# Seven column tiles instead of six accumulate while adaLN's weights stream in; adaLN keeps one PSUM bank

## The chip, the cores and the metric

The kernel runs on one core of a Trainium2 chip. The metric is the device time of one execution, in microseconds, the median of several runs. TensorE multiplies (PE in the profile, its weight loads PEld), VectorE (DVE) and GpSimd (POOL) do elementwise work, ScalarE (ACT) does activations and casts, SyncE (SP) starts every DMA. TensorE writes its sums to PSUM, eight banks of 512 float32 columns on 128 partitions.

## The reference

One layer of a hybrid decoder, in float32, on 2048 prompt tokens and 8 single-token samples. The part that the change touches is the head of it:

```python
shift, scale, gate = adaln(c, w_c, b_c)              # silu(c) @ w_c + b_c, split in three
h = rmsnorm(x, g_pre) * (1.0 + scale[:, None, :]) + shift[:, None, :]
proj = h @ w_in                                      # 2048 -> 5 x 1024
u_a, v_a, z_a, x_b, z_b = jnp.split(proj, [D_A, 2 * D_A, 3 * D_A, 3 * D_A + D_B], axis=-1)
```

Behind it come a gated mixing of chunks of 128 tokens (A), an S5 state space scan (B), a product with `w_out` (2048 x 2048), a second RMSNorm, and the residual. The outputs are the new rows, the normalised v rows of the samples, and the S5 states.

## The kernel before

The tokens are cut into four blocks of 512 (the last has the 8 samples too), the 40 x 128 output columns of `w_in` into column tiles, the 2048 input rows into 16 K tiles (KT). A float32 product is made of three: weights and activations are each split into a rounded high part and the rest (`hi`, `lo`), and `mm3` (lines 95 to 99) multiplies hi by hi, hi by lo and lo by hi. So a K tile of one column tile (`kstep`) is three matmuls of 512 columns. The weights arrive raw by DMA, 512 KB at a time (`wraw`, line 106), and `wpieces` (line 111) makes two pieces of each: ACT casts the high part (line 90), DVE or POOL subtracts it (line 85). A load is either half of one column tile (`whalf`, eight K tiles) or a quarter of two (`wpair`, four K tiles of each).

**The startup** (`startup`, line 1244) cannot make h before adaLN's shift and scale are there, and those need 32 MB of `w_c`: 64 loads of 512 KB (`raw`, eight buffers), four for each of the 16 K tiles. So h is made K tile by K tile, and the first NG = 6 column tiles of the first block accumulate at once, each in a PSUM bank of its own, four of the tag `acc` and two of `aux`. Step s of the loop does four things. Six `kstep`s use K tile s - 2. `ada_ss2` turns the sums of K tile s - 1 (`ada_turn`: four small matmuls into a bank `adat`; DVE adds the biases, lines 289 and 291, into `shiftT` and `GT`), and `hscale` (x times R on DVE, line 342) and `hmake` (ACT: x, line 348, and hi; DVE: lo) make its h. The `w_c` loads of K tile s are multiplied (`ada`, line 271) in two bursts, behind the third and the sixth `kstep`, into a bank `ada` that is opened at the step's start, and `ada_copy` (line 275) takes the sums out to SBUF. Each `ada` starts the load of the buffer that it has freed. The weights of the six column tiles come as pairs through three raw buffers (`wraw2`): loaded in steps 2, 6 and 10, split in steps 4 and 5, 8 and 9, 12 and 13. All this is in `manual_schedule`: each engine, and SP with its DMAs, does its part in the order of the code. An instruction whose buffer is not free yet waits, and what is behind it on its queue waits too.

**Behind the startup** a planner orders the engines by the order of the code and its own estimates. `phase1_rest` does the other column tiles of the block one by one, in two halves of eight K tiles. For each half it calls `half`, which does work that is spread over the tiles: one of 16 steps of the next block's statistics (`stats`: load x, square on ACT, add on POOL, line 338; the 17th call makes R of it, `rms_wide`), from the ninth tile on a share of S5's preparation (`s5_mats`, on POOL above all), and at the ninth tile S5's lanes (`s5_lanes`, on DVE). Then `group_start` begins the next block: its h is made with R (`hgen`, lines 364 to 366) while two column tiles accumulate.

Of the kernel before, what the change touches and what calls it, by code (L numbers as in the profile page):

```python
# [27 lines left out]
G = 64  # L28
GC = 16
P = 64  # L30
KT = D // 128
# [26 lines left out]
def ranges(b):  # L58

    return [(0, TB)] if b < NB - 1 else [(0, 256), (256, 264)]  # L60


class Builder:
# [38 lines left out]
    def wsplit(self, src, raw_pool=None, raw_tag="wraw", raw_bufs=3, pool=None, tags=("whi", "wlo"), bufs=NW, engs=None):  # L102

        return self.wpieces(self.wraw(src, raw_pool, raw_tag, raw_bufs), pool, tags, bufs, engs)

    def wraw(self, src, pool=None, tag="wraw", bufs=3):
        raw = (pool or self.wp).tile([128, 1024], F32, tag=tag, bufs=bufs, name=self.nm("wraw"))
        self.SP.dma_start(raw if len(src.shape) == 2 else raw.rearrange("p (a b) -> p a b", a=2), src)
        return raw
# [1133 lines left out]

    def startup(self, st, NG, ntl):

        I, V, G = self.I, self.V, self.G
        raws, pair = {}, {}
        NS = 4 * KT
        def raw(i):
            if i < NS:  # L1250
                raws[i] = self.wraw(I["wss"][i // 4][:, i % 4 * 4 : i % 4 * 4 + 4, :].rearrange("p k m -> p (k m)"), st, "sraw", NR_)
        ws = [[] for _ in range(NG)]
        def wraw(g, kq):
            pair[g, kq] = self.wraw(self.wpair(I["win"], ntl[1][g], kq), st, "wraw2", 3)
        def wsplit(g, kq):
            a, b = self.wpieces(pair.pop((g, kq)), pool=st, tags=("swh", "swl"), bufs=NG + 2, engs=(V, G))
            ws[g].append(a)
            ws[g + 1].append(b)
        xs = [self.xload(self.hl, "hl", 0, k, NHL) if k < KT - 1 else self.xload(self.tp, "t", 0, k, NT) for k in range(KT)]
        self.constants1()  # L1260
        for i in range(NR_):
            raw(i)
        for g in (0, 2, 4):
            wraw(g, 0)
        ssq = self.tile_()
        for k in range(KT):
            self.stat_add(st, xs[k], ssq, k, TB, V)
        R = self.R[0]
        self.sel = self.cp.tile([128, 9], F32, name="sel")
        V.tensor_add(self.sel, self.ident[:, 0:9], self.ident[:, 32:41])  # L1270
        for i in (64, 96):
            V.tensor_add(self.sel, self.sel, self.ident[:, i : i + 9])
        def ada(ps, i):
            self.ada_mm(ps, raws.pop(i), i % 4)
            raw(i + NR_)
        ps = self.ada_open()
        ada(ps, 0)
        def more():
            ada(ps, 1)
            ada(ps, 2)  # L1280
        self.rms_bcast(ssq, TB, R, more)
        ada(ps, 3)
        V.tensor_scalar(self.bcT[:, 16:32], self.bcT[:, 16:32], 1.0, None, op0=ALU.add)
        sb = self.ada_copy(ps)
        self.hscale(xs[0], R, 0)
        wsplit(0, 0)
        self.ada_ss2(0, sb)
        self.h = [self.hmake(xs[0], 0, 0)]
        wsplit(2, 0)
        ps = self.ada_open()  # L1290
        for q in range(4):
            ada(ps, 4 + q)
            if q == 2:
                wsplit(4, 0)
        sb = self.ada_copy(ps)
        acc = [self.accs(0) if g < 4 else [self.ps.tile([128, 512], F32, tag="aux", bufs=4, name=self.nm("acc"))] for g in range(NG)]
        for s in range(2, KT + 2):
            if s < KT:
                ps = self.ada_open()
            prev = sb  # L1300
            if prev is not None:
                self.hscale(xs[s - 1], R, 0)
            sb = None
            for q in range(NG):
                if q < NG and s >= 2:
                    self.kstep(acc[q], ws[q][0], s - 2, self.h[s - 2], ranges(0), s == 2, s == KT + 1)
                    if (s - 2) % 4 == 3:
                        ws[q].pop(0)
                if q == 1 and prev is not None:
                    self.ada_ss2(s - 1, prev)  # L1310
                if s < KT and q in (2, NG - 1):
                    for a in range(2):
                        ada(ps, 4 * s + q // 3 * 2 + a)
                if s < KT and q == NG - 1:
                    sb = self.ada_copy(ps)
                if q == 2 and prev is not None:
                    self.h.append(self.hmake(xs[s - 1], 0, s - 1))
                if s < KT:
                    if s % 4 == 2 and s < KT - 4 and q % 2 == 0:
                        wraw(q, s // 4 + 1)  # L1320
                    if (s % 4, q) in ((0, 3), (1, 2), (1, 4)):
                        wsplit(0 if q == 3 else q, s // 4)
            if s == KT:
                w = self.wcol(I["win"][ntl[1][NG]])
        return w, acc


    def build(self):
        nc, tc, I, V, G, SP = self.nc, self.tc, self.I, self.V, self.G, self.SP
# [24 lines left out]
        self.R = [self.cp.tile([128, TB + ND], F32, name="R0")]  # L1354
        cm_st, st = self.pool("startup")
        self.constants(st)
        NG = 6
        nta, ntb = self.order(0), self.order(1)
        with tc.manual_schedule():
            w, acc = self.startup(st, NG, nta)  # L1360
# [32 lines left out]
        pair = lambda ntl: lambda hf: [self.wsplit(self.wpair(I["win"], ntl[1][0], 0))] if hf else []  # L1393
# [65 lines left out]
        y, ws = y0, ws0  # L1459
        for b in range(NB - 1):  # L1460
            y, ws = self.phase3(b, ws, y)
        self.lo_engs = [V, V, V, G]
        self.ggr = []
        y, ws = self.phase3(NB - 1, ws, y)
# [75 lines left out]
```

## Time and profile before

| | us |
|---|---|
| median of three runs | 2908.93 |
| lowest and highest | 2904.92, 2912.47 |
| the profiled execution | 2908.74 |
| its span, first to last instruction | 2906.9 |
| TensorE busy in it | 2833.2 (97%) |
| DVE, ACT, POOL busy | 1619.7, 1066.7, 1056.5 |

The profile shows one execution. An engine's busy time counts its instructions from start to end; matmuls overlap in the pipeline, so a busy TensorE may still be slower than it could be, and the distance from one start to the next tells its pace. A line such as `ACT whi L90 <- DMA wraw` says that the instruction of line 90 waited for that transfer. A wait is put down to what came last.

### The profile page before, as it was taken

The page shows a single profiled execution, that of the slowest core. Times are in us where ns is not written, and L with a number is a line of the kernel's source. Part 1 is how long each engine was busy: PE and PEld are TensorE (multiplying, and loading weights), DVE is VectorE, ACT ScalarE, POOL GpSimd, SP SyncE. Part 2 cuts the span into 40 slices and gives each one's busy share as a digit, 9 for nine tenths or more (in the row PEclk, how much of TensorE's full clock was granted, in tenths as well). Part 3 has the DMA queues.
Part 4 walks back from the last instruction along what each step waited for, and adds up shares of the span by engine and source line. Part 5 has one row for each costly group of instructions (what it writes and reads, how often), then busy time and mean ns, then how long its engine had stood idle before and what let it go on. Part 6 is the DMA issues. An engine that isn't in the chain of part 4 may idle for free.

```text
span 2906.9 us, 44350 instructions
## 1 busy us (share of the span) xinstructions
PE 2833.2 (97%) x15804; PEld 2377.5 (82%) x15804; DVE 1619.7 (56%) x2976; ACT 1066.7 (37%) x2008; POOL 1056.5 (36%) x973
## 2 busy tenths in 40 slices
PE   6999999999999999999999999999999999999997
PEld 4676777777999999988888888888888888888986
DVE  4467646557442737465546735582741274473866
ACT  3333444434233232333334332433243343434543
POOL 1128463663341232323232233223234345263442
PEclk9999999999999999999999999999999999999999
DMA  9897988988887373846476565647483365474676
GB/s 356 287 235 203 277 240 236 265 237 235 191 210 202 106 232 127 260 142 201 154 226 192 154 200 179 214 126 234 138 253 102 101 178 177 126 229 120 195 237 219
DMA packets 456559, 581.14 MB, mean 200 GB/s; under 512 B 216593, under 2 KB 303121, under 8 KB 456337
## 3 DMA queue, kind: packets, MB, share of 16 engines
q1 hardware_dynamic: 456338, 578.32, 66.6%
q8 instruction: 124, 2.03, 0.3%
q14 instruction: 97, 0.79, 0.1%
HBM read 466.87 MB, written 102.66 MB: 196 GB/s over the span
## 4 chain that ended last, share of the span: by engine, by line
PE 77%; DVE 11%; DMA 5%; issue 3%; POOL 1%; SPq 1%; ACT 1%; DVEq 0%; ACTq 0%; POOLq 0%
PE acc L97 23%; PE acc L99 22%; PE acc L98 22%; DMA x<-in_xT 2%; DVE wlo L85 2%; DVE Ub L894 2%; PE ada L271 2%; DVE lo L366 1%; DVE x L364 1%; PE mix L526 1%; DVE sct L904 1%; DVE Ub L903 1%; DVE sct L902 1%; PE acc L1223 1%; DVE Ub L905 1%
## 5 line engine op out<-in xcount | busy, mean ns | idle before, releaser
L97 PE MATMUL acc<-hi,whi 128*128 128x512 f32 (+2 forms) x3200 | 1130.0, 355 | 5.4 <-DVE t L85 2.1
L98 PE MATMUL acc<-lo,whi 128*128 128x512 f32 (+2 forms) x3200 | 1120.6, 350 | 11.6 <-DVE lo L366 9.6
L99 PE MATMUL acc<-hi,wlo 128*128 128x512 f32 (+2 forms) x3200 | 1120.1, 350 | 2.3 <-DVE wlo L85 1.9
L85 DVE TENSOR_TENSOR wlo<-wraw,whi 128x512 fp32r<-128x512 f32 x626 | 549.8, 886 | 806.2 <-ACT whi L90 788.5
L90 ACT CAST whi<-wraw 128x512 fp32r<-128x512 f32 x960 | 580.9, 620 | 1115.3 <-PE acc L98 785.6
L85 POOL TENSOR_TENSOR wlo<-wraw,whi 128x512 fp32r<-128x512 f32 x334 | 472.3, 1416 | 1053.6 <-ACT whi L90 955.2
L97 PEld LDWEIGHTS acc<-hi,whi 128*128 128x128 f32 x3200 | 602.4, 189 | 100.5 <-issue 18.2
L98 PEld LDWEIGHTS acc<-lo,whi 128*128 128x128 f32 x3200 | 603.3, 189 | 91.7 <-DVE lo L366 13.7
L99 PEld LDWEIGHTS acc<-hi,wlo 128*128 128x128 f32 x3200 | 602.5, 188 | 89.5 <-DVE wlo L85 4.9
L97 PE MATMUL acc<-yhi,whi 128*128 128x512 f32 (+1 forms) x1024 | 377.5, 369 | 2.8 <-DVE o L1069 2.8
L99 PE MATMUL acc<-yhi,wlo 128*128 128x512 f32 (+1 forms) x1024 | 375.7, 368 | 1.9 <-POOL wlo L85 1.9
L98 PE MATMUL acc<-ylo,whi 128*128 128x512 f32 (+1 forms) x1024 | 376.3, 368 | 0.0
L97 PEld LDWEIGHTS acc<-yhi,whi 128*128 128x128 f32 x1024 | 193.8, 189 | 38.6 <-DVE o L1069 3.6
L99 PEld LDWEIGHTS acc<-yhi,wlo 128*128 128x128 f32 x1024 | 193.3, 189 | 36.5 <-POOL wlo L85 2.5
L98 PEld LDWEIGHTS acc<-ylo,whi 128*128 128x128 f32 x1024 | 193.7, 189 | 34.5 <-issue 0.7
L894 DVE SCALAR_TENSOR_TENSOR Ub<-Ub,apow 128x128 f32<-128x128 f32 (+6 forms) x384 | 143.0, 435 | 2.5 <-ACT Ub L881 2.2
L983 POOL TENSOR_TENSOR sg<-sg,zbl 128x264 f32<-128x264 f32 x64 | 54.7, 854 | 191.1 <-DVE sg L982 133.0
L364 DVE SCALAR_TENSOR_TENSOR x<-x,GT,R 128x512 f32<-128x512 f32 x96 | 88.8, 940 | 31.1 <-DMA x<-in_xT 30.8
L365 ACT ACTIVATE hi<-x,shiftT 128x512 fp32r<-128x512 f32 x96 | 68.5, 723 | 95.0 <-DVE x L364 87.7
L90 ACT CAST hh<-hr 128x264 fp32r<-128x264 f32 x64 | 26.4, 413 | 190.9 <-DMA hr<-Ub 99.7
L1072 POOL TENSOR_TENSOR ossq<-ossq,osq 128x512 f32<-128x512 f32 (+1 forms) x60 | 81.2, 1354 | 32.5 <-ACT osq L1065 32.3
L338 POOL TENSOR_TENSOR ssq<-ssq,t 128x512 f32<-128x512 f32 (+1 forms) x45 | 61.7, 1372 | 83.1 <-ACT t L337 70.8
(286 smaller groups left out, 2798.3 us busy)
## 6 DMA issues: line engine op xcount, KB each, us to landing
wraw<-in_win SPq DMA_DIRECT2D x320, 512.0 KB
wraw<-in_wout SPq DMA_DIRECT2D x128, 512.0 KB
xr<-XB SPq DMA_DIRECT2D x128, 272.0 KB
x<-in_xT SPq DMA_DIRECT2D x128, 256.0 KB
wraw<-in_wss SPq DMA_DIRECT2D x64, 512.0 KB
XB<-t SPq DMA_DIRECT2D x64, 256.0 KB
wraw<-in_wgt SPq DMA_DIRECT2D x32, 512.0 KB
MQ<-qh SPq DMA_DIRECT2D x128, 128.0 KB
```

Source lines behind the costliest of these rows:

```text
L85: eng.tensor_tensor(out, a, b, op=ALU.subtract)
L90: self.S.copy(hi, raw)
L97: mm(acc, whi, xhi, start=start, stop=False)
L98: mm(acc, whi, xlo, start=False, stop=False)
L99: mm(acc, wlo, xhi, start=False, stop=stop)
L271: self.T.matmul(ps[k * 32 : k * 32 + 32, 0:256], self.stat[:, q * 4 + k, :], raw[:, k * 256 : k * 256 + 256], start=q == 0, stop=q == 3)
L338: add_eng.tensor_tensor(ssq[:, 0:n], ssq[:, 0:n], sq[:, 0:n], op=ALU.add)
L364: V.scalar_tensor_tensor(xt, xt, self.GT[:, k, 0:1], R[:, 0:TB], op0=ALU.mult, op1=ALU.mult)
L365: S.activation(hi[:, 0:TB], xt, AF.Identity, bias=self.shiftT[:, k, 0:1])
L894: V.scalar_tensor_tensor(o, i, f, o, op0=ALU.mult, op1=ALU.add)
L983: self.G.tensor_tensor(sg, sg, zb, op=ALU.mult)
L1072: eng.tensor_tensor(ssq[:, 0:nn], ssq[:, 0:nn], sq[:, 0:nn], op=ALU.add)
```

## The change

NG becomes 7, so a seventh column tile accumulates in the startup, in a third bank of `aux`. One bank of `aux` is left for adaLN's sums and their turn, in alternation: `ada_open` moves from the step's start to the first burst, and the first burst moves from behind the third `kstep` to behind the fourth, since the turn of the K tile before must be read first. A burst still is two loads, eight K tiles of `w_c`. The seventh tile has no partner; its weights come in halves: the first is loaded in step 1 and split ahead of the loop, the second is loaded in step 7 and split in step 9. There are ten buffers for split pieces where there were eight. The line that loads pairs (`if s % 4 == 2 and s < KT - 4 and q % 2 == 0: wraw(q, s // 4 + 1)`) is not touched. `phase1_rest` of the first block starts one tile further on.

```diff
         def wraw(g, kq):
-            pair[g, kq] = self.wraw(self.wpair(I["win"], ntl[1][g], kq), st, "wraw2", 3)
+
+            src = self.wpair(I["win"], ntl[1][g], kq) if g < NG - 1 else self.whalf(I["win"][ntl[1][g]], kq // 2)
+            pair[g, kq] = self.wraw(src, st, "wraw2", 3)
         def wsplit(g, kq):
-            a, b = self.wpieces(pair.pop((g, kq)), pool=st, tags=("swh", "swl"), bufs=NG + 2, engs=(V, G))
+            a, b = self.wpieces(pair.pop((g, kq)), pool=st, tags=("swh", "swl"), bufs=NG + 3, engs=(V, G))
             ws[g].append(a)
-            ws[g + 1].append(b)
+            ws[g + 1 if g < NG - 1 else g].append(b)
...
         for q in range(4):
             ada(ps, 4 + q)
+            if q == 0:
+                wraw(NG - 1, 0)
             if q == 2:
                 wsplit(4, 0)
         sb = self.ada_copy(ps)
+        wsplit(NG - 1, 0)
...
         for s in range(2, KT + 2):
-            if s < KT:
-                ps = self.ada_open()
...
                 if q == 1 and prev is not None:
                     self.ada_ss2(s - 1, prev)
-                if s < KT and q in (2, NG - 1):
+                if s < KT and q in (3, NG - 1):
+                    if q == 3:
+                        ps = self.ada_open()
                     for a in range(2):
-                        ada(ps, 4 * s + q // 3 * 2 + a)
+                        ada(ps, 4 * s + q // 4 * 2 + a)
...
                         wsplit(0 if q == 3 else q, s // 4)
+                    if (s, q) == (7, 5):
+                        wraw(NG - 1, 2)
+                    if (s, q) == (9, 5):
+                        wsplit(NG - 1, 2)
...
-        NG = 6
+        NG = 7
```

## Rows read from the trace of the kernel before

**Rows 1.** Busy by stretch: PE, PEld, DVE, ACT, POOL; clock, DMA share, GB/s

```profile
0.00:20.00 20.00, 0.45 (x8) 0.23 (x8) 11.98 (x23) 11.70 (x18) 0.20 (x4) 1.00 0.89 292
20.00:30.00 10.00, 8.53 (x52) 5.26 (x44) 4.85 (x20) 0.00 (x0) 0.00 (x0) 1.00 1.02 379
30.00:40.00 10.00, 7.82 (x63) 4.05 (x64) 5.75 (x10) 5.48 (x10) 4.30 (x3) 1.00 1.04 409
...
40.00:137.00 97.00, 97.00 (x741) 62.69 (x741) 39.32 (x79) 28.75 (x46) 13.20 (x9) 1.00 0.91 332
...
210.00:300.00 90.00, 80.82 (x400) 59.59 (x399) 68.77 (x78) 36.50 (x75) 74.70 (x92) 0.98 0.76 216
```

**Rows 2.** Timeline of TensorE, one step of the startup: start, duration, instruction

```profile
51.63 0.51 PE L282 MATMUL adat<-sel,t 128*128 128x9 f32 x4
...
52.86 1.07 PE L271 MATMUL ada<-wraw,cstat 128*32 128x256 f32 x16
...
54.20 0.39 PE L98 MATMUL acc<-lo,whi 128*128 128x512 f32 x1
54.43 0.40 PE L99 MATMUL acc<-hi,wlo 128*128 128x512 f32 x1
...
59.89 1.07 PE L271 MATMUL ada<-wraw,cstat 128*32 128x256 f32 x16
```

**Rows 3.** Timeline of DVE in the same step

```profile
52.32 0.28 DVE L291 TENSOR_SCALAR GT<-adat,c_bcT,c_gpre 128x9 f32<-128x9 f32 x1
```

**Rows 4.** Waits of SP's queue, 0 to 200 us: total, times, longest

```profile
SPq L108 <- PE ada L271: 59.8, 28, 3.4
```

**Rows 5.** Timeline of SP and ACT: the first pairs' loads and the first cast

```profile
19.43 2.89 SPq L108 DMA_DIRECT2D wraw<-in_win  x3
...
30.91 1.14 ACT L90 CAST whi<-wraw 128x512 fp32r<-128x512 f32 x2 [14.20 <-DMA wraw<-in_win]
```

**Rows 6.** Timeline of POOL, DVE and TensorE, 32 to 41 us

```profile
32.13 1.28 POOL L85 TENSOR_TENSOR wlo<-wraw,whi 128x512 fp32r<-128x512 f32 x1 [31.68 <-ACT whi L90]
...
37.02 0.41 DVE L275 COPY t<-ada 128x256 f32<-128x256 f32 x1
37.36 1.42 DVE L342 TENSOR_TENSOR x<-x,R 128x512 f32<-128x512 f32 x1
...
38.83 0.27 DVE L291 TENSOR_SCALAR GT<-adat,c_bcT,c_gpre 128x9 f32<-128x9 f32 x1
40.64 0.69 DVE L85 TENSOR_TENSOR lo<-x,hi 128x512 fp32r<-128x512 f32 x1 [1.53 <-ACT hi L90]
...
37.96 0.48 PE L97 MATMUL acc<-hi,whi 128*128 128x512 f32 x1
...
38.83 1.07 PE L271 MATMUL ada<-wraw,cstat 128*32 128x256 f32 x16
```

**Rows 7.** Timeline of SP and ACT: a load that is used at once

```profile
257.72 0.38 SPq L108 DMA_DIRECT2D wraw<-in_win  x1
...
260.21 0.62 ACT L90 CAST whi<-wraw 128x512 fp32r<-128x512 f32 x1 [0.28 <-DMA wraw<-in_win]
```

**Rows 8.** TensorE behind a wait: timeline, and busy by stretch as in rows 1

```profile
280.87 0.50 PE L98 MATMUL acc<-lo,whi 128*128 128x512 f32 x1 [2.53 <-DVE lo L366]
...
282.00:285.30 3.30, 3.30 (x14) 1.87 (x13) 3.30 (x4) 0.00 (x0) 3.06 (x4) 0.51 0.64 160
```

**Rows 9.** Timeline of POOL: the split of step 4's pair

```profile
55.23 1.34 POOL L85 TENSOR_TENSOR wlo<-wraw,whi 128x512 fp32r<-128x512 f32 x1 [17.00 <-ACT whi L90]
```

**Rows 10.** Timeline of TensorE and DVE around the next block's R

```profile
256.36 0.50 PE L158 MATMUL ssum<-sqh,ones 128*128 128x512 f32 x1 [0.64 <-ACT sqh L90]
...
271.83 0.69 DVE L145 SCALAR_TENSOR_TENSOR R<-t,R 128x512 f32<-128x512 f32 x1
...
273.05 6.20 DVE L364 SCALAR_TENSOR_TENSOR x<-x,GT,R 128x512 f32<-128x512 f32 x4
...
277.62 0.71 PE L97 MATMUL acc<-hi,whi 128*128 128x512 f32 x2
```

## The prediction

> **What bounds the kernel now.** I read the table of busy time by stretch first, because the change touches one stage. From 40 to 137 us, where six column tiles accumulate beside adaLN, TensorE is busy for all of its 97.00 us [rows 1]. Next the list of what SP's queue waits for: up to 200 us it waits 28 times for adaLN's matmuls, 59.8 us together [rows 4]. So the weight loads run ahead of TensorE and wait for it to give buffers back, and TensorE sets the pace, although the DMA share is 0.91 [rows 1]. The timeline shows the step that repeats: bursts at 52.86 and 59.89 are one step apart, 7.03 us [rows 2]. In it lie 18 matmuls of 512 columns, 0.23 us from start to start (54.20 to 54.43), two bursts of about 1.0 us, a turn of 0.4 us and the passages between them [rows 2]. There is no hole for a seventh tile to fill.
>
> **Part by part. The seventh tile itself: 0.** It brings 48 matmuls, 48 x 0.233 = 11.2 us, into the startup, and takes the same 48 out of the column tiles behind it. A step grows from 7.03 to 7.03 + 3 x 0.233 = 7.73 us. TensorE has no free time to hide them in, so this is a move, not a gain. The count of bursts, turns and passages stays.
>
> **One bank for sums and turn: 0 in a settled step.** A burst may now start only when DVE has read the turn. In the settled step the turn starts at 51.63 [rows 2] and DVE's second sum ends at 52.32 + 0.28 = 52.60 [rows 3], 0.97 us later. In the new order the turn (0.36 us) and two K tiles (2 x 0.7) stand ahead of the burst, 1.8 us, so 0.8 us are spare. Without that cover (DVE held up) the price is whatever DVE is late, and that happens once, next. The Trainium skill (PSUM — Partial Sum Buffer, section PSUM bank collisions raise a hardware error) says that TensorE and VectorE must not touch one bank in the same partitions at once. By that rule the overlap in [rows 6], where the burst and DVE's GT read both start at 38.83, is lost; by the row alone nothing would be lost, and the sum would be 4.8 us smaller, since the burst would not ask for DVE.
>
> **The seventh tile's first weights: 4.8 us.** Its first load is put into SP's order behind the thirteenth adaLN load, and into a pool of three buffers, so it waits for the split of the first pair, whose GpSimd half ends at 32.13 + 1.28 = 33.41 [rows 6]. Then it queues. How long shows the first pair: its load is issued at 19.43 and its cast starts at 30.91 after 14.20 us of waiting [rows 5]. Ahead of it and with it were 16 x of 0.262 MB, eight adaLN loads and itself of 0.524 MB, and 0.17 MB of constants: 9.1 MB. Moved by 30.91 were 20 x 0.292 + 10 x 0.379 + 0.91 x 0.409 = 10.0 MB [rows 1]. So loads land about in order, 0.9 MB behind. For the new load 13.3 MB stand in order (the same, two more pairs, five more adaLN loads, itself), so it lands at 14.2 MB; by 40.00 13.7 MB are moved, hence at 41.1 us.
>
> Its split stands in ACT's, DVE's and GpSimd's order ahead of all that step 2 needs: on DVE behind it wait x times R, both sums, and lo; on ACT hi. From 41.1: cast 0.62, wlo 0.69, x times R 1.42 beside a busy GpSimd (37.36 to 38.78), sums 0.32 (to 38.83 + 0.27 = 39.10) [rows 6]: 44.15, with the gaps between engines 44.3 us. TensorE reaches the burst after two K tiles from 37.96, at 39.5 [rows 6]; it stands there 4.8 us. The K tile of step 3 needs lo, in the trace of before 41.33 - 39.10 = 2.2 us behind the sums [rows 6], so at 46.5; TensorE gets there after a burst, three K tiles and a burst, at 48, so nothing more is late. Bounds: if the load lands as its own bytes end (13.3 MB, 38.9 us) and x times R takes 0.69, 1.9 us; if it lands 1.4 us later, 6.2 us.
>
> **TensorE's clock behind that wait: 1.6 us.** In the trace of before TensorE waits 2.53 us until 280.87, and the granted clock over the 3.3 us from 282.0 to 285.3 is 0.51, that is 1.2 GHz [rows 8]. That loses 1.6 us. The first 40 us of the trace hold the clock at 1.00 through shorter gaps [rows 1], so the bounds are 0 and 1.7. The Trainium skill (TensorE: Matmul & The Clock Gate, section HAM oscillation — how this bites in real kernels) says that an array that stands idle is put back to the half rate; by it 1.6 is due, by the early rows 0.
>
> **Three loads that nobody reads: 2.5 us.** The line that loads a pair in steps 2, 6 and 10 asks for an even q, and q = 6 is now one. So in each of these steps the seventh tile is loaded once more; no split takes these loads (that of step 6 is replaced by the one of step 7). They cost 1.6 MB of DMA, which hides, since TensorE sets the pace. But each needs a fourth buffer of three, which comes free only with the split of the first pair two steps later, and SP's queue stands there, with every adaLN load behind it. That split ends on GpSimd at 55.23 + 1.34 = 56.57 [rows 9], 4.9 us after its turn at 51.63. The eight adaLN buffers last to the end of that step; the next burst is due one step on, 1.8 + 7.7 = 9.5 us after the turn, its second load 0.5 us later. From the release two loads are ahead of its second one: a load alone takes from 257.72 to 260.21, 2.5 us, to be used [rows 7], and each further 0.524 MB at 0.4 MB/us 1.3 us. That is 4.9 + 0.05 + 2.5 + 2 x 1.3 = 10.1 against 10.0: hardly late. With the 0.9 MB lag of the busy start (2.2 us) it is 1.4 us late. Step 7's load waits besides for the dead one to land: 0 to 0.9 more. Three times 0.1 to 1.4 and this: 0.3 to 5.1; I take 2.5, the middle, as neither row is nearer.
>
> **Behind the startup: 5 us.** The statistics of the next 512 tokens are stepped once per half column tile from the first tile behind the startup on, so they now begin and end one tile (11.2 us of TensorE) later against the work that is left; S5's preparation keeps its tile. In the trace of before the sum's matmul runs at 256.36, R is done at 271.83 + 0.69 = 272.5, DVE starts on x at 273.05, and TensorE, through with its last tile at 277.62 [rows 10], waits for lo until 280.87 [rows 8]. So R leads by 5.1 us and is late all the same: 8.4 us lie between it and the first lo. Now the sum's matmul opens the last tile, 277.62 - 11.2 = 266.4, and with the same 16.1 us R comes at 282.5: 10 us later. The last tile has only one pair to split where the one before it had four halves' pieces, so DVE should need less than 16.1 us; at 11, about what R's eleven DVE operations of 0.69 [rows 10] and three subtractions make, it comes at 277.4 and costs 5. Bounds: -2, if the planner that orders this part finds better places, and 10. I take 5, near the middle and from the rows of DVE's own chain.
>
> **The sum** goes against the profiled execution, 2908.74 us (span 2906.9), which is 0.2 us under the median: 4.8 + 1.6 + 2.5 + 5 = 13.9, so 2922.6 us. By the bounds: 0.2 to 23, that is 2909 to 2932.
>
> **Rivals. A, hidden:** the load jumps the queue as the lone one does (2.5 us [rows 7]): issued at 33.5, landed by 36, sums by 39.4, no wait, no clock loss; the dead loads are late by 0.3 and the planner catches the statistics. It decides at a landing of 36.3 us. Time 2909 to 2912, no measurable change. Against it stands the first pair's 11.5 us in the queue [rows 5].
> **B, faster:** behind the startup one tile fewer is to be split and loaded (1.05 MB, four casts, four subtractions) in a stage where TensorE lacks 90.00 - 80.82 = 9.2 us between 210 and 300 [rows 1]. If that goes by more than the startup's prices, the kernel gains; with A's startup and all of it, 2900. It decides where the lost waits pass the 8.9 us of the startup. Against it: what TensorE waits for there is S5's preparation and R, which start no earlier.
> **C, much slower:** S5's lanes, the constants and the statistics all start at the startup's end, and have a tile less to hide behind. If R is the full 10 us late and half again as much falls on S5's preparation, the time is 2908.7 + 8.9 + 15 = 2932.6; it decides where DVE needs all of the 16.1 us again.
>
> **How the numbers follow.** Forecast 0.55, A 0.20, B 0.07, C 0.18. A measurement of this kernel tells about 0.3% from no change, 8.7 us. Of the forecast's spread (+6 to +20) I put three quarters above that, 0.41; with C slower is 0.59. A and the rest of the forecast are same, 0.34; faster is B, 0.07. The range takes in A and C's own time, and leaves out B and what lies beyond C: 2908 to 2933.
>
> **What the profile after would show.** In_win loads 323 instead of 320. A step of 7.7 us. One wait of TensorE of about 5 us near 40 us, with DVE as releaser, at adaLN's burst, and the granted clock at a half behind it. Three waits of SP of some 15 us for a split, and TensorE late at a burst one step later. R done no more than 2 us before the last tile's end. The prediction is wrong if the load lands before 37 us, if TensorE's idle time before the startup's end grows by less than 5 us, or if the stretch from there to the end of the next group's start shrinks.

## The result, and the profile after

The changed kernel takes 2931.76 us (median of four runs, 2929.62 to 2934.45) where the kernel before took 2906.93 beside it (2903.51 to 2912.47). The ratio is 1.0085, with a 95% interval of 1.0072 to 1.0098: 24.7 us slower (21 to 28). The forecast was 2922.6 us, slower, in a range to 2933. The sign and the places were right, and two terms of the sum were far too small. Of all the executions behind this document one, of run 3 below, took 9297 us; it is in no ratio.

The profiled execution of the changed kernel took 2930.59 us, its span is 2928.8 us. From its page, busy time by engine, the group of adaLN's matmuls (busy time and mean, then idle time ahead and its releaser), and the DMA issues:

```profile
PE 2844.1 (97%) x15804; PEld 2380.6 (81%) x15804; DVE 1621.2 (55%) x2974; ACT 1065.8 (36%) x2008; POOL 1050.8 (36%) x975
...
L271 PE MATMUL ada<-wraw,cstat 128*32 128x256 f32 x768 | 63.9, 420 | 28.4 <-DMA wraw<-in_wss 24.4
...
wraw<-in_win SPq DMA_DIRECT2D x323, 512.0 KB
```

The work is the same but for three loads more. To see where the time went, take two marks that both kernels pass: the first accumulator taken out of PSUM (line 397, the startup's end) and a taking out in the second block, behind the group start (line 419). The kernel before:

```profile
140.32 1.63 ACT L397 CAST t<-acc 128x512 fp32r<-128x512 f32 x3
...
439.39 0.59 ACT L419 ACTIVATE t<-acc 128x512 f32<-128x512 f32 x1
```

and the kernel after:

```profile
163.27 1.98 ACT L397 CAST t<-acc 128x512 fp32r<-128x512 f32 x3 [0.26 <-PE acc L99]
...
461.07 0.59 ACT L419 ACTIVATE t<-acc 128x512 f32<-128x512 f32 x1
```

The first mark comes 23.0 us later. Of the seventh tile's 48 matmuls 45, 10.5 us, were moved ahead of it (the last three come behind the first accumulator's end), so the startup has lost 12.5 us. The second mark, behind the same work in both kernels, comes 21.7 us later, so 9.2 us more are lost between the two; behind it the distance stays near 22 to the end. These two numbers are given below for each run, as **startup** and **behind**.

**The startup.** The turn of adaLN's sums (line 282) starts once a step. From turn to turn before: 7.13, then 6.99 to 7.04 in every step. After, from step 2 on: 13.79, 7.73, 7.74, **11.75**, 7.73, 7.72, 7.69, **11.03**, 7.69, 7.73, 7.70, **9.89**, 7.72, 7.72. So ten steps are 7.0 + 0.7 us, as forecast, and four are longer by 6.0 (step 2 takes 7.82 in a run below where nothing waits), 4.0, 3.3 and 2.2 us: 15.5 in all. The loads at the front came through earlier in this execution (TensorE's first wait for them is 17.5 us against 19.6 before), which gives some 2 to 3 us of it back.

TensorE's waits from 20 to 165 us (us in total, times, longest), then SP's up to 170 us, where [rows 4] had 59.8 us for adaLN's matmuls:

```profile
PE ada L271 <- DMA wraw<-in_wss: 6.9, 8, 1.7
PE acc L97 <- DVE GT L291: 3.1, 1, 3.1
```

```profile
SPq L108 <- DVE wlo L85: 54.0, 5, 16.6
...
SPq L108 <- PE ada L271: 23.3, 17, 3.5
```

SP now waits most for a split of weights, 54.0 us, and only 23.3 us for adaLN's matmuls.

Step 2 on TensorE's timeline, ACT's cast of the seventh tile's weights and DVE's sum beside it, and the busy time of the stretch (PE, PEld, DVE, ACT, POOL; clock, DMA share, GB/s):

```profile
34.83 0.61 PE L282 MATMUL adat<-sel,t 128*128 128x9 f32 x4 [1.21 <-DVE t L275]
...
42.63 0.77 PE L97 MATMUL acc<-hi,whi 128*128 128x512 f32 x1 [3.12 <-DVE GT L291]
...
48.62 0.51 PE L282 MATMUL adat<-sel,t 128*128 128x9 f32 x4
```

```profile
39.13 1.14 ACT L90 CAST whi<-wraw 128x512 fp32r<-128x512 f32 x2 [5.63 <-DMA wraw<-in_win]
...
42.22 0.27 DVE L291 TENSOR_SCALAR GT<-adat,c_bcT,c_gpre 128x9 f32<-128x9 f32 x1
```

```profile
42.00:48.30 6.30, 5.67 (x24) 3.25 (x25) 2.21 (x6) 1.43 (x2) 0.00 (x0) 0.50 1.04 398
```

The cast waits for the load, DVE's split and sums come behind it, and TensorE stands 3.12 us until GT is read. Then the granted clock is 0.50, 1.2 GHz, for some six microseconds; the rest of the 6.0, 2.9 us, is that.

The first of the three long steps, on SP, GpSimd and TensorE:

```profile
45.33 1.18 SPq L108 DMA_DIRECT2D wraw<-in_wss  x2
61.33 0.33 SPq L108 DMA_DIRECT2D wraw<-in_win  x1
61.71 13.14 SPq L108 DMA_DIRECT2D wraw<-in_wss  x12
```

```profile
59.95 1.36 POOL L85 TENSOR_TENSOR wlo<-wraw,whi 128x512 fp32r<-128x512 f32 x1 [18.33 <-ACT whi L90]
```

```profile
64.09 0.51 PE L282 MATMUL adat<-sel,t 128*128 128x9 f32 x4
...
67.84 0.64 PE L271 MATMUL ada<-wraw,cstat 128*32 128x256 f32 x8 [1.73 <-DMA wraw<-in_wss]
69.01 1.08 PE L271 MATMUL ada<-wraw,cstat 128*32 128x256 f32 x8 [0.54 <-DMA wraw<-in_wss]
...
75.84 0.51 PE L282 MATMUL adat<-sel,t 128*128 128x9 f32 x4
```

```profile
69.00:72.40 3.40, 3.39 (x14) 2.10 (x15) 0.58 (x1) 0.00 (x0) 1.70 (x2) 0.51 1.03 416
```

SP issues nothing from 46.5 to 61.33. It stands at the unread load, for whose buffer GpSimd's split (59.95 + 1.36 = 61.31) must end. The first adaLN load behind it is issued at 61.71 and used at 67.84. TensorE waits 1.73 and 0.54 us, and then runs 3.4 us at half the clock: 2.3 + 1.7 = 4.0 us.

In the other two of the three TensorE waits less, and the clock stays. The waits of the third, and the busy time of the stretch:

```profile
135.91 0.64 PE L271 MATMUL ada<-wraw,cstat 128*32 128x256 f32 x8 [0.78 <-DMA wraw<-in_wss]
...
137.67 0.64 PE L271 MATMUL ada<-wraw,cstat 128*32 128x256 f32 x8 [1.12 <-DMA wraw<-in_wss]
```

```profile
134.00:140.00 6.00, 4.10 (x29) 2.36 (x29) 2.81 (x4) 3.51 (x6) 3.03 (x2) 1.00 1.01 365
```

The granted clock is 1.00 behind them, and 0.78 + 1.12 = 1.9 of the 2.2 us are waits. In the second of the three it is 1.00 too, behind 0.87 and 0.54 us at the step's first burst and 0.46 and 0.89 us at the next one. That next burst's 1.35 us come from step 7's own load, for which SP stops again until 100.51.

**Behind the startup.** DVE, GpSimd and TensorE around the next block's R (the rows that answer to [rows 10] and [rows 8]):

```profile
290.92 2.93 DVE L85 TENSOR_TENSOR qh<-F,qh 128x512 fp32r<-128x512 f32 x1
293.78 1.88 DVE L144 SCALAR_TENSOR_TENSOR t<-t,t 128x512 f32<-128x512 f32 x1
...
301.55 0.67 DVE L145 SCALAR_TENSOR_TENSOR R<-t,R 128x512 f32<-128x512 f32 x1
```

```profile
291.04 1.15 POOL L761 TENSOR_TENSOR F<-sc,pw 128x576 f32<-128x576 f32 x1
292.15 1.15 POOL L761 TENSOR_TENSOR mu<-sc,pw 128x576 f32<-128x576 f32 x1
293.38 1.73 POOL L762 TENSOR_TENSOR F<-F,mu 128x576 f32<-128x576 f32 x1
```

```profile
279.43 0.50 PE L158 MATMUL ssum<-sqh,ones 128*128 128x512 f32 x1 [1.69 <-ACT sqh L90]
...
300.67 1.08 PE L271 MATMUL ada<-wraw,cstat 128*32 128x256 f32 x8 [2.85 <-DMA wraw<-in_wgt]
308.23 0.79 PE L98 MATMUL acc<-lo,whi 128*128 128x512 f32 x1 [2.04 <-DVE lo L366]
```

```profile
294.00:310.00 16.00, 9.10 (x44) 5.02 (x45) 15.59 (x20) 5.57 (x12) 14.34 (x19) 0.51 0.94 271
```

From the sum's matmul to R it is 279.43 to 302.22, 22.8 us, where it was 16.1 [rows 10]. From 294 to 310 TensorE is busy for 9.1 of 16 us, at half the clock, and DVE and GpSimd for nearly all.

### The profile page after: what moved, and what is told of

Same layout as the page of the kernel before. It is cut to its first block, busy times and chain, and to the rows that moved or that the text cites. A ratio compares the mean times of both kernels' runs of the same rounds, so it can differ in the third digit from the quotient of the medians.

```text
span 2928.8 us, 44378 instructions
## 1 busy us (share of the span) xinstructions
PE 2844.1 (97%) x15804; PEld 2380.6 (81%) x15804; DVE 1621.2 (55%) x2974; ACT 1065.8 (36%) x2008; POOL 1050.8 (36%) x975
## 4 chain that ended last, share of the span: by engine, by line
PE 76%; DVE 10%; DMA 8%; issue 3%; ACT 1%; SPq 1%; POOL 1%; DVEq 0%; ACTq 0%; POOLq 0%
PE acc L97 23%; PE acc L99 22%; PE acc L98 22%; DMA x<-in_xT 3%; DVE wlo L85 2%; DVE Ub L894 2%; DMA wraw<-in_win 1%; PE ada L271 1%; DVE lo L366 1%; DMA wraw<-in_woutr 1%; DVE x L364 1%; DMA wraw<-in_wout 1%; PE mix L526 1%; DMA wraw<-in_wss 1%; DMA xres<-in_xT 1%
## 5 line engine op out<-in xcount | busy, mean ns | idle before, releaser
L85 DVE TENSOR_TENSOR wlo<-wraw,whi 128x512 fp32r<-128x512 f32 x624 | 539.8, 872 | 805.8 <-ACT whi L90 782.8
L364 DVE SCALAR_TENSOR_TENSOR x<-x,GT,R 128x512 f32<-128x512 f32 x96 | 86.9, 920 | 30.2 <-DMA x<-in_xT 29.8
L271 PE MATMUL ada<-wraw,cstat 128*32 128x256 f32 x768 | 63.9, 420 | 28.4 <-DMA wraw<-in_wss 24.4
```

Source lines behind the costliest of these rows:

```text
L85: eng.tensor_tensor(out, a, b, op=ALU.subtract)
L271: self.T.matmul(ps[k * 32 : k * 32 + 32, 0:256], self.stat[:, q * 4 + k, :], raw[:, k * 256 : k * 256 + 256], start=q == 0, stop=q == 3)
L364: V.scalar_tensor_tensor(xt, xt, self.GT[:, k, 0:1], R[:, 0:TB], op0=ALU.mult, op1=ALU.mult)
```

## The experiments

The theory after the comparison: the loss is (1) SP held at three loads that nobody reads, (2) the seventh tile's first weights, which come late, with the half clock behind them, and (3) the statistics, one tile later against the end of the block. The seventh tile and the shared bank cost nothing. Rivals: the bytes of the loads; the bank; the tile that is missing behind the startup, ahead of S5's preparation.

| kernel | ratio to before, 95% interval | us | startup | behind |
|---|---|---|---|---|
| changed kernel | 1.0085 (1.0072 to 1.0098) | +24.7 | 12.5 | 9.2 |
| 1: without unread loads | 1.0058 (1.0044 to 1.0072) | +16.8 | 4.3 | 12.8 |
| 2: all loads, other buffers | 1.0060 (1.0046 to 1.0075) | +17.4 | 2.6 | 9.1 |
| 3: 1, first weights early | 1.0037 (1.0022 to 1.0051) | +10.7 | -1.6 | 9.8 |
| 4: 3, statistics sooner | 1.0022 (1.0012 to 1.0031) | +6.4 | 1.2 | 2.8 |
| 5: six tiles, unread loads half a step early | 1.0104 (1.0088 to 1.0120) | +30.2 | 27.3 | -1.7 |
| 6: six tiles, statistics later | 1.0028 (1.0017 to 1.0039) | +8.1 | -1.2 | 9.0 |
| 7: six tiles, statistics sooner | 0.9995 (0.9987 to 1.0004) | -1.5 | -0.6 | -3.5 |
| 8: six tiles, shared bank | 1.0012 (1.0000 to 1.0024) | +3.5 | -0.5 | 2.4 |
| 9: six tiles, unread loads in place | 1.0057 (1.0043 to 1.0071) | +16.6 | 14.4 | -0.3 |
| 10: 4, three additions on DVE | 0.9991 (0.9981 to 1.0002) | -2.6 | -0.9 | 1.2 |
| 11: 7, three additions on DVE | 0.9988 (0.9980 to 0.9997) | -3.5 | -0.9 | -3.6 |

The third column is what the ratio lies above 1, times the 2904 to 2907 us of the kernel before in the same comparison. The last two are from one execution each, at the two marks; the startup's moves by 2 to 3 us between executions of the same startup (runs 3, 4 and 10). In run 4's, step 2 takes 10.12 us where run 3's takes 7.82: TensorE waits 1.36 us there until 33.35, and its granted clock from 36 to 42 us is 0.52. What lies behind moves by about as much (9.1 to 12.8 in the four runs of seven tiles whose statistics are not moved).

**1. Without the unread loads.**

```diff
-                    if s % 4 == 2 and s < KT - 4 and q % 2 == 0:
+                    if s % 4 == 2 and s < KT - 4 and q % 2 == 0 and q < NG - 1:
```

> The changed kernel without the three loads that nobody reads. My theory: each of them holds SP's queue 13 to 15 us at a buffer that is not free, adaLN's loads queue behind it, and the next step's bursts are late, 4.0 + 3.3 + 2.2 = 9.5 us from turn to turn above the 7.73 of the other steps. So 2931.8 - 9.5 = 2922.3 us (2921 to 2924, since the load of step 7 still waits for a buffer), and those three steps come down to 7.7 to 8 us. Rival, volume: the 1.6 MB themselves are what costs, at 0.4 MB/us 3.9 us: 2927.9. Rival, bank: the bursts are late because sums and turn share a bank: 2931.8, unchanged.

Measured: 2921.3 us, 1.0058. The three steps are 7.74, 7.73 and 7.72 us from turn to turn, and step 2 still takes 13.63. In these steps the forecast 9.5 us come back; by the ratios it is 7.8 us. The three loads cost this, and the step 7 load, which also has to wait for a buffer, costs nothing here.

**2. The same loads in buffers that are free.**

```diff
-            pair[g, kq] = self.wraw(src, st, "wraw2", 3)
+            pair[g, kq] = self.wraw(src, st, "wraw2", 3) if g < NG - 1 else self.wraw(src)
```

> The changed kernel with every load of the seventh tile's weights, the three unread ones too, put into the main pool's three buffers, which stand empty until the startup's end. Nothing is left out: the same bytes move in the same order, but SP no longer waits for a pair's split. My theory (the held queue costs, not the bytes): 2922 us, as without the loads; the seventh tile's first weights stay late, since the place in the order is the same. Rival, volume: 3.9 us above the kernel without them, about 2926 to 2928. Rival, bank: 2931.8.

Measured: 1.0060, the same as without the loads (1.0058), and all steps behind step 2 at 7.7 us. By the ratios alone 3.9 us for the bytes could still hide in the intervals; the steps decide. The 1.6 MB cost nothing there; what costs is that the queue stands. In step 2 the wait for GT is 1.60 us, shorter than 3.12, though the cast of the seventh tile's weights comes at 41.33, later than the 39.13 of the changed kernel. TensorE itself comes to it later: 7.2 us behind the turn (36.04 to 43.24) where it took 4.7 (34.83 to 39.51), since its matmuls there run at half the pace (last section).

**3. The seventh tile's first weights with the first pairs** (beside the edits of 1 and 2).

```diff
-        for g in (0, 2, 4):
+        for g in (0, 2, 4, NG - 1):
             wraw(g, 0)
...
-            if q == 0:
-                wraw(NG - 1, 0)
```

> Without the three unread loads, the seventh tile's loads in the main pool's buffers, and the first of them issued with the first three pairs, ahead of the loads that adaLN's first steps order. My theory: the wait of 3.1 us at the seventh tile's first K tile and the half clock behind it go, together 6.0 us in step 2: 2922.3 - 6.0 = 2916.3 us; up to 1.3 us (0.524 MB at 0.4 MB/us) may come back in step 1, where five adaLN loads now land later: 2915.5 to 2918. Rival: the 0.524 MB more in the busy front cost wherever they stand: 2922, with the wait moved to an earlier burst.

Measured: 1.0037, 6.1 us less than run 1. The wait for GT is gone, step 2 takes 7.82 us, and no burst of the startup waits for its loads. The startup of seven tiles now costs about what that of six does (-1.6 us in this trace, 1.2 in that of run 4, which has the half clock in step 2). What is left is all behind it, 9.8 us in this trace.

**4. Also the statistics sooner.**

```diff
                 if i >= 3:
                     next(st_, None)
+                    if b == 0 and i == NG:
+                        next(st_, None)
```

> As the kernel before this one in the row, and the statistics of the next 512 tokens stepped twice in each half of the first tile behind the startup, so that they stand against the end of the tokens' block where they stood with six tiles. My theory: of what grows behind the startup (9.8 us) most goes: 2916.3 - 9.8 = 2906.5 us, 2906 to 2911. Rival: the tile that is missing behind the startup makes S5's preparation and the constants late, not the statistics: unchanged, about 2916.

Measured: 1.0022. 4.3 us go by the ratios, 7 by the traces, and not 9.8. R is done at 276.9, but now TensorE stands elsewhere:

```profile
285.68 0.65 PE L846 MATMUL pK<-F,bd 128*32 128x128 f32 x8 [6.47 <-POOL F L763]
```

This is S5's preparation, and it waits for GpSimd, which also adds the statistics up. But GpSimd is not busy ahead of F; it stands at a memset, for which the profile names a DMA:

```profile
280.77 0.52 POOL L852 MEMSET ks<- 64x512 f32 x1 [8.66 <-DMA ZB<-t]
```

**5 and 9. The unread loads alone, in the kernel before.** In run 5 they stand right behind the third pair, ahead of the step's last burst:

```diff
                         wraw(q, s // 4 + 1)
+                        if q == 4:
+                            self.wraw(self.whalf(I["win"][ntl[1][NG]], s // 8), st, "wraw2", 3)
```

> The kernel before, six tiles and two banks for adaLN, and in it only the three loads that nobody reads: in steps 2, 6 and 10, behind the three pairs, 0.524 MB of in_win into the pairs' three buffers. My theory: SP stands at each of them until the first pair is split, some two steps later, and adaLN's bursts are late as in the changed kernel: 8 to 12 us above the kernel before, near 9.5. Rival, the shared bank makes these waits: nothing above it here, since sums and turn have a bank each. Rival, volume: 3.9 us above.

In run 9 they stand behind that burst, where the changed kernel has them:

```diff
+                    if s in (2, 6, 10) and q == NG - 1:
+                        self.wraw(self.whalf(I["win"][ntl[1][NG]], s // 8), st, "wraw2", 3)
```

> The kernel before with the three unread loads again, now behind the last burst of steps 2, 6 and 10, where the changed kernel has them; half a step earlier, ahead of that burst, they cost 30 us, three times what was expected. My theory: what decides is how many adaLN loads are issued when SP comes to a stand. Here two more are, which last TensorE half a step (3.5 us) longer, so three times 3.5 us and some half clock go: 8 to 15 us above the kernel before, near the 9.5 us that the three steps lose in the changed kernel. Rival: in a step of six tiles a held queue costs some 10 us wherever the load stands: 25 to 30 us above, and then the changed kernel's smaller loss has another reason.

Measured: 30 us in run 5, three times what was expected, and 16.6 in run 9 (12 to 21 by the interval), just above the 8 to 15 expected. Both have two banks for adaLN, so the bank doesn't make these waits. From turn to turn the three steps take 16.04, 16.52 and 16.70 us in run 5 and 12.18, 12.51 and 12.16 in run 9, where the others take 7.0. SP and TensorE in run 5:

```profile
55.46 0.34 SPq L108 DMA_DIRECT2D wraw<-in_win  x1
55.90 16.82 SPq L108 DMA_DIRECT2D wraw<-in_wss  x14
```

```profile
51.74 1.07 PE L271 MATMUL ada<-wraw,cstat 128*32 128x256 f32 x16
60.94 1.08 PE L271 MATMUL ada<-wraw,cstat 128*32 128x256 f32 x8 [5.85 <-DMA wraw<-in_wss]
```

and in run 9:

```profile
55.19 0.33 SPq L108 DMA_DIRECT2D wraw<-in_win  x1
55.57 8.88 SPq L108 DMA_DIRECT2D wraw<-in_wss  x10
```

```profile
54.73 1.07 PE L271 MATMUL ada<-wraw,cstat 128*32 128x256 f32 x16
61.78 0.94 PE L271 MATMUL ada<-wraw,cstat 128*32 128x256 f32 x8 [3.23 <-DMA wraw<-in_wss]
```

SP is released at nearly the same time in both, 55.46 and 55.19 us. In run 5 the loads in hand last to the burst of 51.74, in run 9 to the one of 54.73, half a step on. The wait is 2.6 us shorter, and less is lost to the clock. In the changed kernel the loads stand as in run 9, but its two steps are 1.4 us longer together, and the wait is 1.73: again 1.5 less. So much the same time explains all three: from the issue of the first adaLN load behind the stop to its use 5.0 to 6.2 us pass here (55.90 to 60.94, 55.57 to 61.78, 61.71 to 67.84; 5.0 to 6.4 over all nine stops of the three kernels), and what the loads in hand don't cover of that TensorE waits for.

**6. The statistics one tile later, in the kernel before.**

```diff
-                if i >= 3:
+                if i >= 3 and (b or i > NG):
```

> The kernel before with the statistics of the next 512 tokens begun one column tile later, with the second tile behind the startup; S5's preparation and the constants keep their place and the startup is untouched. My theory: that alone makes R late at the end of the block and costs 7 to 10 us (7.1 us less lay behind the startup in the trace of the seven tile kernel with its statistics put back, 9.8 in all). Rival, one tile fewer behind the startup makes S5's preparation late: here no tile is missing, so nothing above the kernel before.

Measured: 1.0028, 8.1 us (4.9 to 11.3), as forecast, with no tile missing. Its rows are like those of the changed kernel, on TensorE and on DVE:

```profile
266.29 0.39 PE L158 MATMUL ssum<-sqh,ones 128*128 128x512 f32 x1
...
284.78 1.08 PE L271 MATMUL ada<-wraw,cstat 128*32 128x256 f32 x8 [2.48 <-DMA wraw<-in_wgt]
...
306.84 0.50 PE L98 MATMUL acc<-lo,whi 128*128 128x512 f32 x1 [2.17 <-DVE lo L366]
```

```profile
287.29 0.67 DVE L145 SCALAR_TENSOR_TENSOR R<-t,R 128x512 f32<-128x512 f32 x1
```

R is done 15.4 us later than before (272.52), 21.7 us behind the sum's matmul.

**7. The statistics sooner, in the kernel before** (the edit of run 4, with six tiles).

> The kernel before with the statistics of the next 512 tokens stepped twice in each half of the first tile behind the startup, so that they end one tile sooner. My theory: R is then done some 15 us ahead of the last tile's end instead of 5.1, and the wait of 2.53 us for lo with the 1.6 us of half clock behind it goes: up to 4.1 us below the kernel before. Rival: GpSimd, which does these additions, is what S5's preparation waits for in the same stretch (a wait of 6.5 us for it stands in the trace of the seven tile kernel with its statistics put back), so the additions that come sooner cost as much there: no change, or up to 4 us above.

Measured: 0.9995, no change clear of noise. The second mark comes 4.1 us sooner, 3.5 of it behind the startup. That is near the 4.1 us forecast, but in part by luck: the wait of 2.53 us for lo is gone, and in its place TensorE waits 2.84 us for hi at 283.42, since DVE waits 5.62 us for a load of x. By the interval the whole kernel is between 3.8 us faster and 1.2 slower.

**8. The shared bank alone, in the kernel before.**

```diff
+        held = self.ps.tile([128, 512], F32, tag="aux", bufs=4, name=self.nm("held"))
+        self.T.matmul(held[:, 0:9], self.ident, self.sel, start=True, stop=True)
...
-                if s < KT and q in (2, NG - 1):
+                if s < KT and q in (3, NG - 1):
+                    if q == 3:
+                        ps = self.ada_open()
```

> The kernel before, six tiles, with the one bank left for adaLN alone: a tile of PSUM is held through the startup and read at its end, sums and turn share the last bank, and the first burst of a step stands behind the fourth K tile instead of the third, as in the changed kernel. My theory: the burst is ready when its turn is read, so no change, within 0.2% of the kernel before (up to 2 us for the first steps). Rival: in each of the 14 steps TensorE stands until DVE has read the turn, 0.4 us or more each: 5 us or more above.

Measured: 1.0012 (1.0000 to 1.0024). By the time alone it is 0 to 7 us. The trace decides: steps of 7.00 to 7.03 us behind a first of 7.13, the startup 0.5 us shorter, no wait of a burst. In one step, turn and burst on TensorE and DVE's second sum:

```profile
51.14 0.51 PE L282 MATMUL adat<-sel,t 128*128 128x9 f32 x4
...
53.07 1.07 PE L271 MATMUL ada<-wraw,cstat 128*32 128x256 f32 x16
```

```profile
51.83 0.28 DVE L291 TENSOR_SCALAR GT<-adat,c_bcT,c_gpre 128x9 f32<-128x9 f32 x1
```

DVE has read the turn at 52.11, 0.96 us ahead of the burst. What is over in the time lies behind the startup, where this kernel is the kernel before.

**10 and 11. Three of the additions on DVE**, with seven tiles (on top of run 4) and with six (on top of run 7):

```diff
-                self.stat_add(self.xp, self.xload(self.xp, "xst", b, i, 2), ssq, i, n, G)
+                self.stat_add(self.xp, self.xload(self.xp, "xst", b, i, 2), ssq, i, n, V if b == 1 and i < 4 else G)
```

> Seven tiles without the unread loads, with the early first load and with the statistics stepped twice in the first tile behind the startup, and the additions of its first three of these steps given to DVE instead of GpSimd. My theory: what is left above the kernel before (6.4 us) is GpSimd's: its additions and S5's preparation stand closer together, and TensorE waits for GpSimd's F. With three additions of some 1.5 to 2 us taken from it: 4 to 6 us of that go, 2905 to 2908 us. Rival: S5's preparation is late since its constants and lanes have one tile less ahead of them, whoever adds: unchanged, 0.2% above the kernel before.

> The kernel before with the statistics stepped twice in the first tile behind the startup and their first three additions given to DVE. A candidate to beat both kernels. My theory: the group start behind the block comes 4.1 us sooner with the early statistics (that was seen), and GpSimd, freed of the additions, gives the rest of S5's preparation no reason to be late: 3 to 5 us below the kernel before. Rival: DVE, which splits the weights in the same tile, is as full: no change, within 0.1%.

Measured: 0.9991 with seven tiles, 9 us less than run 4 (an estimate from the two intervals: 5 to 13) where 4 to 6 were expected, and the wait of 6.47 us for F is gone. The additions are not all that differs: the planner has put two of F's multiplications ahead of the memset that GpSimd waits at. The first of them, and the memset, on GpSimd:

```profile
267.81 1.15 POOL L761 TENSOR_TENSOR F<-sc,pw 128x576 f32<-128x576 f32 x1
...
276.32 0.52 POOL L852 MEMSET ks<- 64x512 f32 x1 [6.24 <-DMA MT<-ks]
```

0.9988 with six tiles (0.9980 to 0.9997), 3.5 us below the kernel before: the lowest ratio here, and just outside of what chance gives to one comparison; among eleven it can be chance. With the same repairs six and seven tiles take the same time within the intervals.

## Why the prediction was right or wrong

The time lies in the range, and the sign is right, but the change of 24.7 us is above the 0.2 to 23 that the forecast's own bounds allow. The range reaches it because it took in rival C's time. The terms, one by one:

**Seventh tile 0, shared bank 0: right.** The step is 7.73 us as forecast, run 8's trace shows no wait for the bank, and runs 10 and 11 take the same.

**The first weights 4.8 and the clock 1.6: right in sum (6.4 against 6.0; run 3 gave back 6.1), by luck, and wrong in place and in parts.** The cast came at 39.13 where 41.1 was forecast, since the first pairs came earlier in that execution. The wait was not at the burst but one instruction later, at the seventh tile's first K tile: the first burst did not wait, so it had a bank that was still free, and the seventh accumulator had to wait for the turn's (read from the order of the waits). And the wait was 3.1 us, the half clock cost 2.9: one part too large, the other too small. The Trainium skill (TensorE: Matmul & The Clock Gate, section HAM oscillation — how this bites in real kernels) says that an array that stands idle is put back to the half rate. The trace agrees where the waits are long: 0.50 behind the 3.12 us, and 0.51 behind the 1.73 and 0.54 us. It shows no fall behind shorter ones: 1.00 behind 0.87 and 0.54, and behind 0.78 and 1.12 us. The early rows, by which the prediction's lower bound was 0, hold more than shorter gaps: TensorE's first wait there is 19.6 us, and the clock reads 1.00 behind it.

**Three unread loads 2.5: right in mechanism, mis-sized; 9.5 us by the trace, 7.8 by the ratios.** The split ended 4.96 us after its turn (4.9 forecast), and the burst was due 9.8 us after it (9.5). What failed is the time of a load behind the release: I took 3.9 us for the first, from a load that was used 2.5 us after its issue in an emptier stage [rows 7], and kept the lag of the busy start as the upper bound, of which I took half. (That bound of 1.4 us does not follow from its terms either: 10.1 and the lag of 2.2 are 12.3, 2.3 behind the 10.0.) Measured from the release are 6.5, 5.6 and 5.5 us in the three steps (61.33 to 67.84, 96.27 to 101.86, 130.39 to 135.91). The load of step 7 cost 1.35 us of waits where 0 to 0.9 were taken. And behind the first of these waits TensorE runs at half the clock again, 1.7 us: the term for the clock was counted once, and it was due twice.

**Behind the startup 5: right in mechanism, mis-sized; 9.2 us by the trace, 8.1 in run 6, which does this one thing.** The sum's matmul was forecast for 266.4 and came there (279.43 less the startup's 12.5 is 266.9). The step that failed is the chain from it to R: 11 us, since fewer splits stand beside it. It was 22.8. In the trace of before the chain's operations take 0.69 us each [rows 10], and GpSimd does nothing from 263.5 to 273.4 us; moved by one tile, the chain runs beside GpSimd at work on S5's preparation, and an operation takes 1.88, its neighbour 2.93. The Trainium skill (SBUF — State Buffer, section Who interferes with whom) says that a VectorE instruction with two inputs from SBUF and a GpSimd instruction that reads SBUF contend for a shared read port, and that the order of issue decides who is kept out. The rows above agree in that DVE's 2.93 ends at 293.85 and its 1.88 at 295.66, each about 0.55 us after GpSimd's instructions end (293.30, 295.11); which of the two issued first they do not tell. No run takes GpSimd's work away from beside the chain, so this reading of the 22.8 us is not tested by itself.

**The rivals.** C gave 2932.6, nearest to the time, and its condition came true: DVE needed more than the 16.1 us again. Its prices were not those measured (8.9 for the startup, which lost 12.5, and 15 behind it, where 9.2 were lost). A needed the lone load's speed, which the queue didn't give. B's gain from the tile that is missing doesn't show in any run.

**What stays open:** why taking three additions from GpSimd was worth 9 us with seven tiles and 2 with six. GpSimd's time is not shown to be the cause: ahead of F it stood 8.66 us at the memset in run 4, and in run 10 two of F's multiplications come ahead of that memset, so the gain may be the new order's. The wait of 6.47 us that they remove is from one execution of run 4, the longest of its twelve (2918 us; the median is 2911), so some of it may be that execution's own.

## What to carry to other kernels

When one engine issues all loads, a load into a buffer that is not free is a stop for everything behind it: price it by what the loads in hand still cover when the queue starts again, with the queue's own measured time from release to use, not by its bytes. When a piece of work moves between stages, look at what was stepped once per piece: it moves against its deadline, and it lands beside other work, which can change the price of its instructions. And a wait can have half the clock behind it: take that as a bound for each wait by itself, for here it came behind two of the startup's four late places and not behind the other two.

## What the runs showed of the hardware that was not expected

- TensorE waited for 1.73 and 0.54 us and then had a granted clock of 0.51 for 3.4 us; behind 3.12 us it was 0.50 for some 6 us. Behind 0.78 and 1.12 us it stayed 1.00 (134 to 140 us).
- In run 2 the matmuls between 37.49 and 39.20 us start 0.43 us apart, the pace of the half clock, while the row for 36 to 42 us gives a granted clock of 1.00. Which of the two is off there is not settled.
- A load of 512 KB behind another one is used 6.1 us after its issue when the queue starts from empty (61.71 to 67.84), and 5.0 to 6.4 us over the nine stops of the changed kernel and runs 5 and 9, although the DMA share from 69 us on is 1.03.
